# Attention scores, q times k transposed: the stores move from SyncE's queue to ScalarE's

## Chip, cores, metric

One Trainium2 chip, one core of it. The metric is the device time of one execution in microseconds (us), as a median of several executions. The core's span in the profile is some 1.9 us shorter than the device time. The TensorE clock granted in the profiled runs at full size was 0.77 to 0.86 of full speed.

## The reference

```python
# q, k: [8, 8, 512, 64] float32
scale = 1.0 / np.sqrt(64)
return (np.einsum('bhqd,bhkd->bhqk', q, k) * scale).astype(np.float32)   # [8, 8, 512, 512]
```

It reads 16.8 MB and writes 67.1 MB.

## The kernel before

The 8 x 8 heads are done in 4 units of 16 heads. Each unit loads k and q (two DMAs of 2.1 MB), GpSimd casts them to bf16, TensorE transposes them, and 4 output tiles of 4.2 MB are computed. A tile is eight pairs of matmuls into PSUM, evacuated in turn by ScalarE and VectorE into one big SBUF buffer, and then one store. Three big buffers serve the loads and the output tiles alike; so the fourth load waits for a cast, and the third output tile waits for the cast of the fourth load.

```python
big_pool = ctx.enter_context(tc.tile_pool(name="big", bufs=3))
psum_pool = ctx.enter_context(tc.tile_pool(name="psum", bufs=2, space=bass.MemoryType.PSUM))
...
def evacuate(dst, src):                       # pinned: keeps the program's order on its engine
    if n_evac % 2 == 0:
        pinned(nc.scalar.mul(out=dst, in_=src, mul=scale))
    else:
        pinned(nc.vector.tensor_scalar(out=dst, in0=src, scalar1=scale, ...))
...
def load_and_cast(v):
    xf = big_pool.tile([P, 2, 2, J * D], f32, name="big")
    for x, src in enumerate((k_r, q_r)):
        nc.sync.dma_start(out=xf[:, x], in_=src[v]...)
    ...                                       # four casts on GpSimd
...
def scores(v, t):
    kT, qz = ts[v]
    o = big_pool.tile([P, 2, RO, S], f32, name="big")
    for x in range(2):
        for i in range(0, RO, 2):
            ps = psum_pool.tile([P, 2, S], f32, name="ps")
            ...                               # two matmuls
            evacuate(o[:, x, i:i + 2, :], ps)
            yield
    nc.sync.dma_start(out=out_r[v, t], in_=o.rearrange("p x i k -> p x (i k)"))
...
cast = [load_and_cast(v) for v in range(UNITS)]   # all loads are first in the order
```

## Time and profile before

| | before |
|---|---|
| device time, median (range) | 202.59 us (202.53 to 202.62) |
| span in the profile | 200.7 us |
| busiest compute engine | VectorE, 53% of the span |
| data queue q1 | 98.3% of 16 DMA engines' span |
| DMA rate over the span | 418 GB/s |

In the profile's page, a line of a group gives busy time, mean and the idle time before it. A wait line gives total us, number and longest. A queue line gives packets, MB and the share of the 16 DMA engines' time that its packets took. The lines on which the argument rests are in the prediction below.

### The profile page before, as it was taken

The page shows a single profiled execution, that of the slowest core. Times are in us where ns is not written, and L with a number is a line of the kernel's source. Part 1 is how long each engine was busy: PE and PEld are TensorE (multiplying, and loading weights), DVE is VectorE, ACT ScalarE, POOL GpSimd, SP SyncE. Part 2 cuts the span into 40 slices and gives each one's busy share as a digit, 9 for nine tenths or more (in the row PEclk, how much of TensorE's full clock was granted, in tenths as well). Part 3 has the DMA queues.
Part 4 walks back from the last instruction along what each step waited for, and adds up shares of the span by engine and source line. Part 5 has one row for each costly group of instructions (what it writes and reads, how often), then busy time and mean ns, then how long its engine had stood idle before and what let it go on. Part 6 is the DMA issues. An engine that isn't in the chain of part 4 may idle for free.

```text
span 200.7 us, 1143 instructions
## 1 busy us (share of the span) xinstructions
PE 105.3 (52%) x384; PEld 45.8 (23%) x384; DVE 106.8 (53%) x98; ACT 85.0 (42%) x97; POOL 39.5 (20%) x22
## 2 busy tenths in 40 slices
PE   0035758566657465478637496748585667510000
PEld 0034535223214131224313122312121111100000
DVE  6705538486475976485749357844444444630000
ACT  2004423864755629253844384366435243620000
POOL 1299999995000000000000000000000000000000
PEclk9999576999699999957999759975858858975555
DMA  6999999999999999999999999999999999999994
GB/s 206 424 444 437 421 421 441 434 395 421 434 424 441 428 431 431 433 426 434 431 428 424 434 441 424 431 431 434 424 431 434 431 424 431 428 437 428 428 428 199
DMA packets 5509, 83.95 MB, mean 418 GB/s; under 512 B 384, under 2 KB 384, under 8 KB 384
## 3 DMA queue, kind: packets, MB, share of 16 engines
q1 hardware_dynamic: 5504, 83.89, 98.3%
q8 instruction: 3, 0.05, 0.1%
q14 instruction: 2, 0.02, 0.0%
HBM read 16.78 MB, written 67.11 MB: 418 GB/s over the span
## 4 chain that ended last, share of the span: by engine, by line
DMA 40%; DVE 10%; PE 8%; ACT 6%; issue 1%; ACTq 0%; SPq 0%; DVEq 0%
DMA out_dram<-big 40%; DVE big L68 9%; PE ps L141 8%; ACT big L66 5%; ACT qz L103 1%; DVE qz L103 1%; ACTq L66 0%; SPq L146 0%; DVEq L68 0%
## 5 line engine op out<-in xcount | busy, mean ns | idle before, releaser
L141 PE MATMUL ps<-kT,qz 128*128 128x512 bf16 x256 | 87.6, 447 | 55.5 <-ACT big L66 41.6
L68 DVE TENSOR_SCALAR big<-ps 128x1024 f32<-128x1024 f32 x64 | 78.4, 1224 | 59.8 <-PE ps L141 37.2
L66 ACT ACTIVATE big<-ps 128x1024 f32<-128x1024 f32 x64 | 65.5, 1023 | 73.0 <-PE ps L141 37.2
L141 PEld LDWEIGHTS <-qz 128*128 128x128 bf16 x256 | 27.2, 106 | 111.0 <-issue 97.5
L89 POOL CAST xb<-big 128x2048 bf16<-128x2048 f32 x16 | 38.8, 2468 | 7.9 <-DMA big<-in_k_dram 7.3
L117 PE MATMUL tp<-identity,xb 128*128 128x128 f32 x64 | 11.6, 346 | 13.4 <-POOL xb L89 13.4
L103 ACT COPY kT<-tp 64x512 f32<-64x512 f32 x16 | 9.2, 577 | 15.3 <-PE tp L117 15.1
L103 DVE COPY kT<-tp 64x512 f32<-64x512 f32 x16 | 11.0, 686 | 6.3 <-PE tp L117 6.0
L117 PEld LDWEIGHTS tp<-identity,xb 128*128 128x128 f32 x64 | 10.5, 184 | 15.2 <-POOL xb L89 13.4
L103 DVE COPY qz<-tp 64x512 f32<-64x512 f32 x16 | 11.0, 687 | 2.7 <-PE tp L125 2.5
L103 ACT COPY qz<-tp 64x512 f32<-64x512 f32 x16 | 9.6, 602 | 2.9 <-PE tp L125 2.7
L125 PE MATMUL tp<-identity,xb 128*128 128x128 f32 x64 | 9.4, 300 | 2.5 <-ACT kT L103 2.5
L125 PEld LDWEIGHTS tp<-identity,xb 128*128 128x128 f32 x64 | 8.5, 156 | 4.3 <-issue 3.3
L156 DVE MEMSET qz<- 128x4096 uint32 x2 | 6.9, 3472 | 2.5 <-PEq L184 1.7
L103 ACT ACT_TABLE_LOAD x1 | 1.3, 1283 | 0.7 <-PEq L184 0.7
masks.py:199 POOL TENSOR_SCALAR_AFFINE_SELECT identity<-identity 128x128 f32<-128x128 f32 x1 | 0.3, 292 | 0.1
masks.py:197 POOL MEMSET identity<- 128x128 f32 x1 | 0.2, 204 | 0.3 <-POOLq L184 0.3
L184 POOL MEMSET const-float32-0.0<- 128x1 f32 x1 | 0.1, 98 | 0.2 <-issue 0.2
L184 POOL MEMSET const-bfloat16-1.0<- 128x1 bf16 x1 | 0.1, 101 | 0.0
L184 POOL MEMSET const-uint8-127<- 128x1 uint8 x1 | 0.1, 101 | 0.0
L184 POOL MEMSET const-float32-1.0<- 128x1 f32 x1 | 0.1, 98 | 0.0
## 6 DMA issues: line engine op xcount, KB each, us to landing
out_dram<-big SPq DMA_DIRECT2D x16, 4096.0 KB, 20.7
big<-in_k_dram SPq DMA_DIRECT2D x4, 2048.0 KB, 18.1
big<-in_q_dram SPq DMA_DIRECT2D x4, 2048.0 KB, 22.7
```

The source lines that it names most:

```text
L66: pinned(nc.scalar.mul(out=dst, in_=src, mul=scale))
L68: pinned(nc.vector.tensor_scalar(out=dst, in0=src, scalar1=scale, scalar2=None, op0=mybir.AluOpType.mult))
L89: pinned(nc.gpsimd.tensor_copy(out=xb[:, :, s].rearrange("p (g i) d e -> p g e i d", i=wide), in_=xf[:, x, s].rearrange("p (g e i d) -> p ...
L103: pinned(copy(out=dst(s, h), in_=src[:, h]))
L117: pinned(nc.tensor.transpose(out=tp[:, j, :], identity=identity, in_=kb[:, j0 + j]))
L125: pinned(nc.tensor.transpose(out=tp[:, i, jj, :], identity=identity, in_=qb[:, RO * jj + i0 + i]))
L141: pinned(nc.tensor.matmul(out=ps[:, w, :], lhsT=qz[:, i + w, n, :], rhs=kT[:, n].rearrange("d m s j -> d (m s j)"), start=True, stop=True))
L156: nc.vector.memset(qz, 0.0)
L184: nc = _bacc.Bacc("TRN2", target_bir_lowering=False, num_devices=1)
```

## The change

The intent is to give the stores a hardware queue of their own, so that they don't stand behind the loads, and to let an engine issue them that has just finished its own part of the tile.

```diff
@@ def scores(v, t):
                 evacuate(o[:, x, i:i + 2, :], ps)
                 yield
-        nc.sync.dma_start(out=out_r[v, t], in_=o.rearrange("p x i k -> p x (i k)"))
+
+        pinned(nc.scalar.dma_start(out=out_r[v, t], in_=o.rearrange("p x i k -> p x (i k)")))
```

## The prediction

> **What bounds the kernel now.** I read the page's slices and queues first, then the stretches, then the waits of the two queues concerned, and last the timeline of the stretch in which loads and stores meet. The strip of 40 slices and the queue table:
>
> ```profile
> DMA  6999999999999999999999999999999999999994
> GB/s 206 424 444 437 421 421 441 434 395 421 434 424 441 428 431 431 433 426 434 431 428 424 434 441 424 431 431 434 424 431 434 431 424 431 428 437 428 428 428 199
> ...
> q1 hardware_dynamic: 5504, 83.89, 98.3%
> ```
>
> The reader should see that the DMA engines have work in every slice, that only the first and last slices are partly empty, and that all loads and stores go through one hardware queue, q1. No compute engine is above 53% of the span. Next, the stretches (columns: length, busy time and count of PE, PEld, DVE, ACT, POOL, then clock, DMA share, GB/s):
>
> ```profile
> 0.00:5.00 5.00, 0.00 (x0) 0.00 (x0) 3.34 (x1) 1.28 (x1) 0.70 (x6) 1.00 0.63 206
> 5.00:41.00 36.00, 18.41 (x80) 12.45 (x81) 17.94 (x20) 12.90 (x18) 32.02 (x14) 0.86 1.01 430
> 41.00:198.00 157.00, 86.88 (x304) 33.38 (x303) 85.52 (x79) 70.83 (x79) 6.78 (x3) 0.81 1.00 429
> 198.00:200.70 2.70, 0.00 (x0) 0.00 (x0) 0.00 (x0) 0.00 (x0) 0.00 (x0) 0.50 0.10 42
> ```
>
> Loads (mostly before 41 us) and stores (after) move at the same 430 and 429 GB/s, at a full DMA share. The time is bytes over rate: 83.89 MB / 0.430 MB per us = 195 us, plus about 1.5 us before the first packet, 2.5 us after the last, and some 1.7 us of small dips. One 4.19 MB store takes 9.75 us of the engines, one 2.10 MB load 4.88 us. Then the waits, first on SyncE's queue, then on ScalarE (total us, times, longest):
>
> ```profile
> SPq L146 <- DVE big L68: 152.5, 16, 17.6
> ...
> ACT big L66 <- DMA out_dram<-big: 31.3, 12, 3.5
> ```
>
> SyncE issues each store as soon as VectorE finishes a tile's last evacuation; it blocks nobody while it waits. ScalarE waits 12 times, 2.6 us in the mean, for a store to give back one of the three big buffers: that is the DMA pushing back on the compute. It shows that a small delay of ScalarE has somewhere to vanish.
>
> **What the Trainium skill says.** DMA: Bandwidth & Descriptors, section "Issuing engines are not separate DMA queues": DMAs of any issuing engine run on the same 16 DMA engines and interleave, and issuing from several saves only sequencer time. The trace cannot test the interleaving (it has one data queue), but the sequencer time it would save is small here: 0.37 us per store on a SyncE that is idle otherwise. The same page, "Queues, rings and completion order": each DMA engine takes turns between the queues that have work, one packet at a time. No run of before shows it; my main risk rests on it. The same page, "Where 436 GB/s comes from", has 435 GB/s as the fabric ceiling; 430 GB/s measured agrees, and says that no reordering of queues has much above it to gain. Perfetto Trace Analysis, "DMA Instruction — HWDGE (DVE, Sync)": the reported time of such an instruction ends when the sequencer is free, without the data movement. The trace agrees: 0.37 us on SyncE against a median of 20.7 us to landing. So ScalarE would be held for tenths of a microsecond per store, not for ten.
>
> **The change part by part.**
>
> *Removed:* nothing from the DMA engines; the same 16 stores in the same form. SyncE loses 16 issues, of no worth, because it is on no path.
>
> *Added on ScalarE:* 16 issues at SyncE's 0.37 us (I assume the same on ScalarE), 6 us on an engine that is busy for 85 of 201 us. And each issue must wait in ScalarE's program order for VectorE's eighth evacuation of the tile, so ScalarE's first evacuation of the next tile can no longer run ahead of it. In the timeline of before it does so at a few places: ScalarE begins an evacuation at 63.63 us while that tile's predecessor is stored at 64.24. Cost there: 0.61 + 0.37, about 1 us of ScalarE. In the steady part it is hidden: the store at 91.97 us would free ScalarE at about 92.35, and its next evacuation starts at 92.72 anyway, on a landing. Even an unhidden microsecond does not reach the DMA: the median store needs 20.7 us to land for 9.75 us of data, so about one whole store is queued ahead of it.
>
> *Moved:* the order in which bytes go. Now store 0 is issued at 36.81 us behind the last loads and must let them finish. On its own queue it starts at once and shares the engines with them. Here are the stores, and the last load's cast with what follows it:
>
> ```profile
> 36.81 0.40 SPq L146 DMA_DIRECT2D out_dram<-big  x1
> ...
> 47.49 0.39 SPq L146 DMA_DIRECT2D out_dram<-big  x1
> ...
> 56.55 0.37 SPq L146 DMA_DIRECT2D out_dram<-big  x1
> ...
> 64.24 0.37 SPq L146 DMA_DIRECT2D out_dram<-big  x1
> ```
>
> ```profile
> 43.17 4.86 POOL L89 CAST xb<-big 128x2048 bf16<-128x2048 f32 x2 [0.26 <-DMA big<-in_q_dram]
> ...
> 48.07 1.02 ACT L66 ACTIVATE big<-ps 128x1024 f32<-128x1024 f32 x1 [3.44 <-PE ps L141]
> 48.16 1.22 DVE L68 TENSOR_SCALAR big<-ps 128x1024 f32<-128x1024 f32 x1 [0.74 <-POOL xb L89]
> ```
>
> GpSimd casts the last load (q of unit 3) as soon as it lands; the third output tile takes that load's buffer, so both evacuating engines start it at 48.07, when the cast ends at 48.03. Landings, from the DMA view of narrow windows: the last k load 18.33 + 19.6 = 37.9, the last q load 18.70 + 24.3 = 43.0, store 0 36.81 + 17.1 = 53.9, store 1 47.49 + 16.0 = 63.5.
>
> Now the sum for after. ScalarE has copies until 37.16 in its order ahead of the first issue, so store 0 goes out at about 37.2; its first packet follows some 0.75 us later (the first load is issued at 0.74 us and the DMA share begins near 1.5), so 37.95. The last q load has 43.0 - 37.95 = 5.05 us of transfer left. At half rate it takes 10.1 us and lands at 48.0 instead of 43.0. Its two casts (4.86 us) end at about 52.9 instead of 48.03, and tile 2 starts 4.9 us later. It took 56.55 - 48.07 = 8.5 us to fill, so its store is issued at about 61.4 and has packets at 62.2. Store 0 and the load together have the same bytes as before, so store 0 lands at 53.9 still and store 1 at 63.5. The last store of all is issued at 178.1 and lands 21.8 us later, 199.9, while the packets end near 198.2, so a landing is some 1.6 us behind the last packet and the queue runs dry at 63.5 - 1.6 = 61.9. **The gap: 62.2 - 61.9 = 0.3 us.** The reserve of store 2 (before: 61.9 - 57.3 = 4.6 us) is just used up. After that it grows back: tiles fill in 7.7 to 8.7 us and a store takes 9.75, about 1 to 2 us per tile, and tile 3's store, issued at about 69.7, has until 72.0. At the end the last store is still behind a full queue, so the end moves by the gap alone.
>
> The sum: 202.6 + 0.3 = **202.9 us**.
>
> **The rivals.**
> (A) *The turns are not equal.* If stores get two packets to the load's one, the load needs 3 x 5.05 = 15.1 us and lands near 53, tile 2's store comes near 66.4 with packets at 67.2, and the DMA engines starve for about 5 us: 208 us, 2.5% slower. For it: nothing in the trace; against: loads and stores have packets of one size (5504 packets for 83.89 MB, of which 384 are tiny, so 16 KB each), and an equal turn of equal packets is an equal share. If the load is favoured, or stays first because descriptors are served in the order of issue, nothing is lost: 202.6 us.
> (B) *ScalarE becomes the bound.* It would take an issue that holds it for several microseconds, or its wait for VectorE falling on the path. For it: the waits column of SyncE is long (152.5 us), and the waiting now happens on a working engine. Against: nearly all of that is simply the time in which VectorE and ScalarE fill the tile together; ScalarE adds to its own work only the last evacuation of VectorE, at most 1.2 us, plus 0.37 us, per 9.75 us tile. Even wholly exposed, 8.7 + 1.6 = 10.3 us per tile for the longest fills alone would cost about 0.5 us each for some of 16: 204 to 206 us.
> (C) *A mixture of reads and writes moves faster*, since the two directions might overlap in an engine. At most the 5 us of overlap would shrink, by perhaps 1 us: 201.7 us. Against: 430 GB/s in both directions, near the ceiling named above. A store that starts earlier is by itself no gain, because the DMA engines had no gap to fill there.
>
> **Range and chances.** The central case is 202.9. Down to 201.9 for (C), up to 204.8 for an unequal share or some exposed ScalarE delay. The limits at 2% are 198.5 and 206.7: the first needs 4 us that no gap of the DMA strip offers (chance 0.01); the second needs most of (A) or all of (B) (0.05). Same: 0.94.
>
> **What would show it.** Right: two data queues, with 16.8 and 67.1 MB; DMA share at 9 in all inner slices, at most a slight dip near 60 to 65 us; the last q load landing near 48, its casts ending near 53, store 2 issued near 61.4; ScalarE's issues of about 0.4 us; its waits for landings a little shorter, with the store issues in them; mean DMA rate still near 418 GB/s. Wrong: a last load that lands at 43 (no sharing) or past 50 (unequal), a hole in the DMA strip in the steady part, a tile period above 9.75 us with ScalarE's wait for VectorE on the chain, or a rate in the shared stretch clearly above 430 GB/s.

## The result, and the profile after

| | before | after |
|---|---|---|
| device time, median (range) | 202.56 us (202.41 to 202.62), 4 runs | 203.01 us (202.94 to 203.07), 4 runs |
| span in the profile | 200.7 us | 201.2 us |
| last q load: issue to landing | 18.70 + 24.3 = 43.0 | 18.78 + 26.8 = 45.6 |
| casts of the last q load end | 48.03 | 50.62 |
| store 0, 1, 2, 3 issued at | 36.81, 47.49, 56.55, 64.24 | 36.66, 48.53, 59.38, 67.50 |

Executions over 1.5% slower than the fastest of the same kernel are left out of the means. The ratio is 1.0023, with a 95% interval of 1.0006 to 1.0041: the same within 2%, but a little slower, clear of the noise. Ratios here are the mean time of one kernel's fast runs over that of the other's of the same rounds, so they are not quite the ratios of the medians.

The strip and the queue table of the page after the change:

```profile
DMA  6999999999999999999999999999999999999993
GB/s 205 430 449 420 427 443 430 404 414 433 414 433 446 423 417 446 435 415 436 440 423 417 446 433 420 433 440 430 417 433 446 417 420 453 427 417 427 427 446 156
...
q10 hardware_dynamic: 4352, 67.11, 78.0%
q1 hardware_dynamic: 1152, 16.78, 20.2%
```

There are two data queues now, and the strip is as full as before. The stretch in which I had feared a hole, after the change (length, busy time and count of each engine, clock, DMA share, GB/s):

```profile
50.00:56.00 6.00, 3.77 (x8) 1.07 (x8) 2.45 (x2) 5.04 (x7) 0.61 (x1) 0.54 1.00 423
56.00:62.00 6.00, 3.60 (x13) 1.15 (x12) 3.67 (x3) 2.38 (x4) 0.00 (x0) 0.89 1.02 437
62.00:68.00 6.00, 4.28 (x22) 2.07 (x21) 3.67 (x3) 3.03 (x4) 0.00 (x0) 1.00 1.02 437
```

No hole: 437 GB/s on both sides of 62 us. The cast of the last q load, and ScalarE's own timeline with its queue (ACTq), after the change:

```profile
45.77 4.85 POOL L89 CAST xb<-big 128x2048 bf16<-128x2048 f32 x2 [2.80 <-DMA big<-in_q_dram]
```

```profile
36.66 0.42 ACTq L147 DMA_DIRECT2D out_dram<-big  x1
38.00 1.02 ACT L66 ACTIVATE big<-ps 128x1024 f32<-128x1024 f32 x1 [1.29 <-POOL xb L89]
...
48.53 0.38 ACTq L147 DMA_DIRECT2D out_dram<-big  x1
50.65 1.02 ACT L66 ACTIVATE big<-ps 128x1024 f32<-128x1024 f32 x1 [5.08 <-POOL xb L89]
...
59.38 0.38 ACTq L147 DMA_DIRECT2D out_dram<-big  x1
59.86 1.02 ACT L66 ACTIVATE big<-ps 128x1024 f32<-128x1024 f32 x1 [1.46 <-DVE big L68]
```

Two things are to be seen. GpSimd now waits 2.80 us for the load instead of 0.26, and tile 2 starts at 50.65 instead of 48.07. And behind store 2, ScalarE's next evacuation has waited 1.46 us for VectorE: it is held by the issue that stands ahead of it. The waits of ScalarE after the change show how often:

```profile
ACT big L66 <- DMA out_dram<-big: 13.5, 6, 2.9
ACT big L66 <- DVE big L68: 11.3, 6, 2.5
ACT big L66 <- POOL xb L89: 9.4, 3, 5.1
```

Before, ScalarE waited 31.3 us in 12 waits for landings. Now it waits six times for landings and six times for VectorE's last evacuation, 24.8 us together. By these numbers one wait has taken the place of the other, and the DMA rate is the same.

**Which engine ends last.** Each of the 16 DMA engines ends its part of a transfer with a 4-byte packet, so the trace gives 16 end times for each transfer. I took the median and the last of them, for the last load, for store 0 and for the last store (us from the span's start):

| run | last q load: median, last | store 0: median, last | last store: median, last | span |
|---|---|---|---|---|
| before | 42.25, 42.67 | 51.97, 53.39 | 198.09, 199.49 | 200.7 |
| after | 44.03, 45.27 | 51.98, 53.66 | 198.07, 199.98 | 201.2 |

The median DMA engine ends at the same time in both kernels. The 0.5 us lie in the one engine that ends last. It is not one and the same engine throughout. After the change, the engine that is last at store 0 (53.66) can be followed through its packets in steps of 9.72 us to 150.85, at store 10; there another one is already later, at 151.06. The last engine is behind that of the kernel before by 0.27 us at store 0, 0.18 at store 8 and 0.49 at the end. So in this trace part of the 0.5 us arises long after the last load. The experiments ask where the cost comes from.

### The profile page after: what moved, and what is told of

The parts are those of the page before. It is cut to its first block, busy times and chain, and to the rows that moved or that the text cites. A ratio compares the mean times of both kernels' runs of the same rounds, so it can differ in the third digit from the quotient of the medians.

```text
span 201.2 us, 1129 instructions
## 1 busy us (share of the span) xinstructions
PE 103.5 (51%) x384; PEld 44.7 (22%) x384; DVE 106.8 (53%) x98; ACT 85.0 (42%) x97; POOL 39.5 (20%) x22
## 5 line engine op out<-in xcount | busy, mean ns | idle before, releaser
L117 PE MATMUL tp<-identity,xb 128*128 128x128 f32 x64 | 9.8, 308 | 13.5 <-POOL xb L89 13.5
L117 PEld LDWEIGHTS tp<-identity,xb 128*128 128x128 f32 x64 | 9.1, 164 | 15.0 <-POOL xb L89 13.5
L125 PE MATMUL tp<-identity,xb 128*128 128x128 f32 x64 | 10.2, 317 | 2.5 <-ACT kT L103 2.5
L125 PEld LDWEIGHTS tp<-identity,xb 128*128 128x128 f32 x64 | 9.2, 165 | 4.1 <-POOL xb L89 2.7
```

Of the source, the lines that this page charges most:

```text
L117: pinned(nc.tensor.transpose(out=tp[:, j, :], identity=identity, in_=kb[:, j0 + j]))
L125: pinned(nc.tensor.transpose(out=tp[:, i, jj, :], identity=identity, in_=qb[:, RO * jj + i0 + i]))
```

## The experiments

Theory S: the cost comes from store 0 and the last load sharing the DMA engines. Rival I: it comes from ScalarE's issues in the other 15 tiles. Rival L: it is only the accident of which DMA engine is last.

### Store 0 alone, and all but store 0, from ScalarE

```diff
-        nc.sync.dma_start(out=out_r[v, t], ...)
+        if v == 0 and t == 0:          # the second run: if (v, t) != (0, 0)
+            pinned(nc.scalar.dma_start(out=out_r[v, t], ...))
+        else:
+            nc.sync.dma_start(out=out_r[v, t], ...)
```

> Only store 0 goes out from ScalarE; the other 15 stay on SyncE. The change costs 0.45 us (203.01 against 202.56). If that cost comes from the stretch in which loads and stores share the DMA engines, this run has all of it: 203.0 us, last q load landing near 45.6 as in the changed kernel. If it comes from ScalarE issuing in the steady part, this run has none: 202.55 us. If it is only which DMA engine happens to be last (in the changed kernel the slowest engine ends 1.9 us after the median engine, before 1.4 us, the medians being equal at 198.1), the time is anything from 202.3 to 203.3 and follows that distance.

> Store 0 stays on SyncE behind the loads; the other 15 go out from ScalarE. Sharing theory: the last q load lands at 43.0 as before, store 2 is issued near 57, 202.55 us. ScalarE-issue theory: 203.0 us. Last-engine theory: 202.3 to 203.3, following the distance of the slowest DMA engine from the median one. In all three the 15 issues lengthen ScalarE's tile in the unhidden places by some 0.4 us each without moving the end.

Measured, five runs each: store 0 alone 203.15 us (202.66 to 203.27), ratio to before 1.0021 (1.0008 to 1.0035). All but store 0: 202.56 us (202.35 to 202.72), ratio 0.9998 (0.9985 to 1.0012).

| run | last q load: median, last | store 0: median, last | last store: median, last | span |
|---|---|---|---|---|
| store 0 alone | 44.01, 44.90 | 52.34, 54.36 | 198.41, 200.18 | 201.4 |
| all but store 0 | 42.14, 42.55 | 51.86, 53.22 | 198.06, 199.38 | 200.6 |

The cost is there with store 0 alone and gone with the other fifteen, so I falls. L as a mere accident is unlikely, because the time follows the place of store 0. S fits, but these two runs show only that the cost goes with store 0's queue, not that the sharing makes it. How the cost shows differs too. With store 0 alone, the median engine is already 0.37 us late at the end of store 0 (52.34 against 51.97) and stays so; in the changed kernel only the last one is late.

The median's part can be read from the packets. In each run some 16 KB packets of the loads are slow in the 6 us after store 0's issue. The table has what those over 0.65 us took beyond the usual 0.61, per DMA engine, and the end of store 0 (the last two runs follow below; one trace each):

| run | slow packets, us per engine | store 0, median end |
|---|---|---|
| before | 0.37 | 51.97 |
| after | 0.40 | 51.98 |
| store 0 alone | 0.66 | 52.34 |
| all but store 0 | 0.26 | 51.86 |
| tiny early store | 0.79 | 52.37 |
| later place | 0.46 | 52.07 |

The two columns differ from before by the same amounts within 0.1 us, so by these traces the slow packets account for the delay of the median engine. They are there before the change too, and why they are slow is open.

### Is a new queue slow to start?

In the changed kernel store 0 is issued at 36.66, but its first packet starts at 40.46. The DMA view of two windows, by queue, after the change, the first 37 to 40 us and the second 40 to 43:

```profile
q1 hardware_dynamic: 74, 1.16, 97.6%
```

```profile
q1 hardware_dynamic: 42, 0.69, 60.1%
q10 hardware_dynamic: 31, 0.51, 39.5%
```

For over three microseconds after the issue the store's queue q10 moves nothing. The next experiment uses ScalarE's queue once, early, with a tiny store to a scratch tensor:

```diff
+    scratch = nc.dram_tensor("scratch", [P, 16], bf16, kind="Internal").ap()
+    pinned(nc.scalar.dma_start(out=scratch, in_=qzs[1][:, 0, 0, :16]))
```

> The changed kernel with one tiny store (32 bytes of each of 128 rows to a scratch tensor) issued from ScalarE near 9 us, so that its queue has been used before store 0. In the changed kernel store 0 is issued at 36.66 and its first packet starts only at 40.46, 3.8 us later, so the load lost 2.6 us and not the 5 I predicted. If a first use of the queue costs those 3 us, the first packet of store 0 now starts within 1 us of its issue, near 37.5, and the last q load lands near 48. If what was already handed to the DMA engines goes first, the first packet still starts near 40.5 and the load lands near 45.6. Time 203.0 in the second case, up to 203.3 in the first.

Measured: 202.99 us (202.55 to 203.14), ratio 1.0013 (0.9999 to 1.0026). Store 0 was issued at 37.43 and its first packet started at 41.69, 4.3 us later; the last load's cast began at 45.27. So it is not the first use of the queue. Nor is ScalarE's queue slow by itself: with two big buffers (a run below), when all loads have landed, store 0 is issued at 46.76 and its first packet starts at 47.70, 0.94 us later.

### An early store beside a deep queue of loads

```diff
+    scratch = nc.dram_tensor("scratch", [P, RO * N * P], bf16, kind="Internal").ap()
+    pinned(nc.scalar.dma_start(out=scratch, in_=qzs[1].rearrange("p i n q -> p (i n q)")))
```

> The changed kernel with an extra store of 2.10 MB (16 KB of each of 128 rows to a scratch tensor) issued from ScalarE near 9.4 us, when SyncE's queue holds some 9.5 MB of loads. Time: 2.10 MB / 0.430 = 4.9 us more, 207.9, in every theory. Where its packets lie tells how the two queues take turns. Equal turns at once: first packet near 10.5, last near 20.3. A fixed amount already handed to the DMA engines goes first (some 5 to 6 packets of 0.61 us each, as at store 0), then equal turns: first packet near 13.2, last near 23. Order of issue across the queues: first packet near 31, after all loads issued before it.

Measured: 207.94 us (207.82 to 208.04), as expected from 4.9 us more of bytes. The store was issued at 9.44, its first packet started at 13.17, its last transfer packet was done by 24.02. The DMA view of 9.5 to 13 us, then of 13 to 23 us:

```profile
q1 hardware_dynamic: 93, 1.36, 103.7%
```

```profile
q1 hardware_dynamic: 152, 2.15, 51.6%
q10 hardware_dynamic: 136, 2.10, 48.9%
```

This settles how the queues take turns here. For 3.7 us only the loads run, some six packets of 0.61 us for each DMA engine. After that the turns are equal, 51.6% to 48.9%. It is neither equal turns at once, as I had predicted, nor the order of issue, with which the store's first packet would have come near 31 us. In the changed kernel the last load had some 5.6 us of packets left when store 0 was issued at 36.66 (before, its median engine ends at 42.25). Of these 3.8 us ran undisturbed, and the other 1.8 took twice as long: the median engine ended 1.8 us later, at 44.03. The last engine, and with it the landing, came 2.6 us later, not the 5.0 of the prediction.

### When compute sets the pace

The DMA bound hides ScalarE's part. To see it bare, I halved the stores (output wrong: half of it is not written), from SyncE and from ScalarE:

```diff
-  .dma_start(out=out_r[v, t], in_=o.rearrange("p x i k -> p x (i k)"))
+  .dma_start(out=out_r[v, t][:, 0], in_=o[:, 0].rearrange("p i k -> p (i k)"))
```

> The kernel before, but each store writes only the first half of its tile (2.10 MB; half of the output stays unwritten, wrong on purpose). The DMA engines then need 50.3 MB / 0.430 = 117 us and compute sets the pace: store 0 still near 36.8, then 15 tiles at the 7.7 to 8.5 us that a fill takes, 36.8 + 15 x 8.1 = 158, plus some 7 us of the last store and 2 outside the span: about 167 us. If fills themselves are paced by landings and are shorter when unhindered, less, down to 155.

> The changed kernel with the same half stores. In its full-size trace an unhindered tile took 8.12 us from store issue to store issue against 7.69 before, and the next 9.23 against 8.53: 0.43 to 0.70 us more. If ScalarE's issue with its wait for VectorE is a real cost that only the DMA bound hides, this run is 15 x 0.43 to 0.70 = 6 to 10 us slower than the half stores from SyncE, about 3 to 6%. If ScalarE's issue costs nothing by itself, the two are equal.

Measured, in fast runs: from SyncE 163.29 and 163.77 us (two other runs, of 168.1 and 168.3 us, were slow, and the profile is of one of them); from ScalarE 178.12 and 180.05 us (two others, of 181.2 and 184.5 us, were slow). Over the full-size kernel before, the ratios are 0.8072 and 0.8840, so ScalarE's is 0.8840 / 0.8072 = 1.095 times SyncE's. That is more than the 3 to 6% expected, and the reason given there is not what the trace shows. A half store needs only the first four evacuations (store 0 from SyncE goes out at 32.40 here, against 36.81 for the whole one), and they are long done; ScalarE's timeline has the issue 0.06 us behind the start of an evacuation, and beside it:

```profile
99.77 1.02 ACT L66 ACTIVATE big<-ps 128x1024 f32<-128x1024 f32 x1 [0.47 <-PE ps L141]
99.83 0.34 ACTq L147 DMA_DIRECT2D out_dram<-big  x1
```

So ScalarE does not wait for VectorE's last evacuation there. By the traces, store 2 goes out 4.2 us later (55.59 against 51.40); the last q load, which shares the engines with the stores, lands at 48.0 instead of 43.0. From store 2 to store 15 the tiles take (171.17 - 55.59) - (159.22 - 51.40) = 7.8 us longer, 0.6 us each. (One trace is fast, the other slow; the slow one is the quicker kernel, so the sign is safe and the size is not.) I first thought of the place of the issue in ScalarE's order and moved it behind the next tile's first evacuation:

```diff
-        pinned(nc.scalar.dma_start(...))      # at the end of the tile
+                if (x, i) == (0, 0):
+                    store()                   # the tile before, behind this tile's first evacuation
```

> Half stores from ScalarE, each placed one evacuation later in ScalarE's order: behind the first evacuation of the next tile. Half stores from ScalarE were 15 us (9%) slower than from SyncE in fast runs; in the traces 4.2 us of it lie before store 2 (loads and stores share the engines and tile 2 waits for the last load's casts) and 0.6 us in each later tile. If the 0.6 us come from where the issue stands between ScalarE's evacuations, this run loses only the early part: some 168 us. If they come from ScalarE issuing at all, it stays near 179 us.

> The half stores from SyncE once more, for a profile in the fast state (the first one fell in a run of 168.1 us while the fast ones took 163.3 and 163.8) and on the chip of the two other runs: 163.5 us in fast runs, with a tile every 7.7 to 9.3 us.

Measured in fast runs: the later place 186.8 to 188.9 us (one slow run of 191.6), ratio 0.9251; SyncE again 162.9 and 163.6 us, ratio 0.8056 (two slow runs of 166.1 and 167.5; its profile is one of them again). The later place is not better but worse, 1.148 times SyncE's: my expectation missed on both branches. The last experiment leaves the half stores on SyncE and adds a tiny store on ScalarE in the same place of its order, from a constant tile:

```diff
         nc.sync.dma_start(out=out_r[v, t][:, 0], ...)
+        pinned(nc.scalar.dma_start(out=scratch[v * TILES + t], in_=identity[:, :4]))
```

> Half stores from SyncE as before, and after each of them a tiny store (16 bytes of each of 128 rows of a constant tile) issued from ScalarE in the place where the changed kernel has its store. It takes the same kind of issue on ScalarE (some 0.34 us of its sequencer) but depends on no evacuation and frees no buffer. The half stores from ScalarE were 15 us slower than from SyncE, the later place 24 us slower. If an issue on ScalarE by itself disturbs the alternation of the two evacuating engines, this run is slow too, 172 us or more. If what the store waits for or what it moves in the order of loads and stores is the cost, it stays at the 163.5 us of the half stores from SyncE.

Measured in fast runs: 163.72 and 165.26 us (two slow ones of 167.3 and 168.4), ratio 0.812 (0.8075 to 0.8166), as SyncE alone. So an issue of this length in ScalarE's order costs nothing measurable here by itself. The real store differs in more: it shares with the loads, and it leaves later in its tile than SyncE's does (at 99.83, some 2.6 us after the end of the fourth evacuation). The same late moment from SyncE was not tried. What the real store's issue on ScalarE does to a compute-bound kernel stays open; what the traces show is that both evacuating engines wait longer for TensorE. These are the half stores from SyncE (a slow run), then from ScalarE:

```profile
ACT big L66 <- PE ps L141: 47.9, 46, 2.1
...
DVE big L68 <- PE ps L141: 33.2, 42, 1.8
```

```profile
ACT big L66 <- PE ps L141: 59.8, 51, 2.8
DVE big L68 <- PE ps L141: 44.2, 44, 3.4
```

The granted clock differed too (0.96 and 0.98 in SyncE's two fast runs of the first call, 0.92 and 0.93 in ScalarE's, 0.85 to 0.87 with the later place). The clock alone does not explain the difference: ScalarE's fast run of 178.1 us at 0.93 is 10 us longer than SyncE's slow ones of 168.1 and 168.3 us at 0.90 and 0.89. Whether the rest of the clock's difference is a cause or a consequence, the runs can't tell.

### Without the reserve of a queued store

Whole stores again, but two big buffers instead of three, from SyncE and from ScalarE:

```diff
-    big_pool = ctx.enter_context(tc.tile_pool(name="big", bufs=3))
+    big_pool = ctx.enter_context(tc.tile_pool(name="big", bufs=2))
```

> The kernel before with two big buffers instead of three: no store is queued ahead. Tile 0 must wait for the casts of the third load (near 38 us), store 0 near 46.5, and each tile then costs a fill (7.7 to 8.5 us) plus issue-to-packet (0.75) plus the landing behind the last packet (1.6), about 10.4 us instead of 9.75: 47 + 16 x 10.4 + 2 = 215 us, with holes in the DMA strip.

> The changed kernel with two big buffers. If the reserve of a queued store is what hides ScalarE's 0.4 to 0.7 us per tile, this run is 15 x 0.4 to 0.7 = 6 to 10 us slower than two buffers with SyncE. If the wait for the buffer's landing hides it (ScalarE issues about 1.5 us before the landing that lets it go on anyway), the two are equal within 1 us, near 215 us.

Measured: from SyncE 216.59 us (215.92 to 217.55), from ScalarE 218.31 us (218.15 to 218.90). The ratios to before are 1.0695 and 1.0786, so ScalarE's is 1.0085 times SyncE's, about 1.8 us. (It is not the clock: SyncE's runs at the lowest, 0.77 and 0.78, took 215.9 and 217.2 us.) It lies between the two theories and nearer to the second: most of ScalarE's delay falls into the wait for the landing, a rest of about 0.1 us per tile does not. ScalarE's waits for landings, of the two in the same order:

```profile
ACT big L66 <- DMA out_dram<-big: 44.6, 14, 4.7
```

```profile
ACT big L66 <- DMA out_dram<-big: 44.5, 14, 5.3
```

ScalarE waits as long and as often for the landing, whoever issues. With the third buffer back, the same difference of 1.8 us is gone, as the run with all stores but store 0 on ScalarE shows (202.56 against 202.53 us).

### A later place at full size

> The changed kernel at full size with the same later place of the issue. Where DMA sets the pace the place does not matter: 203.0 us as the changed kernel, 202.5 if the later store 0 (issued at about 39 instead of 36.7, so less sharing) takes back what the sharing cost.

Measured: 202.80 us (202.55 to 203.51), ratio 1.0021 (1.0001 to 1.0041). It can't be told from the changed kernel nor, within some tenths, from before. It shares less: store 0 is issued at 37.83, its first packet starts at 41.87, and the median engine ends the last q load at 42.94 (44.03 in the changed kernel, 42.25 before). Yet the mean is not lower, so the cost does not visibly follow the length of the sharing. No version here is faster than the kernel before. With a DMA strip that is full from end to end, none was expected to be by much.

## Why the prediction was right, point by point

- **The bound.** Right. The DMA engines move 83.9 MB at 430 GB/s in both kernels; the rates of the stretch from 80 to 198 us are 429 and 429 GB/s.
- **ScalarE's issue takes 0.37 us.** Right: 0.38 us for most, 0.42 for the first.
- **The issue holds ScalarE until VectorE is done, and that is hidden.** Right, and more frequent than "a few places": six waits of 11.3 us. The run with all but store 0 on ScalarE shows it costs nothing at the end; that the third buffer's reserve is what hides the last of it is shown by the pair with two buffers.
- **Store 0 "starts at once and shares the engines".** Wrong. It starts 3.8 us after its issue and only then takes equal turns, as the early store shows with 3.7 us and 51.6% to 48.9%. So every time that followed was too late: the last q load landed at 45.6 and not at 48.0, its casts ended at 50.62 and not at 52.9, store 2 was issued at 59.38 and not at 61.4. The fill of tile 2 itself took 59.38 - 50.65 = 8.7 us for the 8.5 I used.
- **The gap of 0.3 us.** Wrong. The queue does not run dry: by the median engine store 1 ends at 61.70 and store 2 has been issued 2.3 us before that. Two readings were loose as well. The 5.05 us that the load was to have left run to its landing at 43.0, not to its last packets at 42.25 to 42.67; and the landing 1.6 us "behind the last packet" holds for the median engine only: before the change the last engine ends at 199.49, 0.4 us before the landing at 199.9.
- **The sum, 202.9 us.** Right in size, 203.01 measured, and right that nothing big would move; that its last term fits is luck. The 0.3 us of starving did not happen, and in their place there are 0.45 us that come with store 0 on the second queue, as the run with store 0 alone shows. That the sharing itself makes them is not shown. With store 0 alone and with the tiny early store the median engine ends 0.3 us late, by slow packets; in the changed kernel only the DMA engine that ends last is late, and why is open.
- **Rival (A), unequal turns.** The turns are unequal at the beginning, in the load's favour, so nothing starved. **Rival (B)** happened off the path that sets the end. **Rival (C)**, a faster mixture: no. From 40 to 43 us the changed kernel moved 1.20 MB, the kernel before 1.13; over 36 to 48 us the two are within 1%.

## What to carry to other kernels

The DMA strip here was full from end to end, and moving the stores to another queue only changed the order of the bytes. In such a case look first for a hole that the move could fill, and if there is none, expect little. Then look at what the reordering delays: the load that shared with a store landed 2.6 us later, and store 2, which waited for its buffer, went out 2.8 us later, of 4.6 us of reserve. Letting an engine that computes issue the stores was safe here while the DMA engines set the pace; with half stores, where they did not, the same move cost 9%, for reasons that stay open.

## What the Trainium skill lacked or had wrong

- DMA: Bandwidth & Descriptors, "Queues, rings and completion order" has the engines take turns between queues by packets. True here (51.6% to 48.9%) only after the first 3.4 to 4.3 us: until then a store issued on a second queue beside queued loads moved nothing, while some six 16 KB packets of the loads ran on each engine. The page does not have this head start.
- The same page, "Issuing engines are not separate DMA queues", says that issuing from several engines saves sequencer time. It has nothing on what the move of the issues to a computing engine can cost: 9.5% in the run with half stores. The sequencer time alone is not the reason, since a tiny store in the same place cost nothing there (0.812 against 0.8056).
- No page that I read has a 16 KB instruction packet holding back the data of one DMA engine. Before the change the last engine is behind the median one by 0.42 us at the last load, 1.42 us at store 0 and 1.40 us at the end. An instruction packet of 0.96 us, at 48.4 us, lies within store 0, and the data packet that starts as it ends took 0.98 us instead of 0.61. With two big buffers from SyncE, where the queues run empty between stores, the lag is 0.07 to 0.24 us, but 0.9 to 1.9 us at stores 4, 6, 7, 12 and 13; instruction packets lie at 95 to 99, 116.4 and 177.7 us, within stores 4, 6 and 12. That they cause the lag fits each time, but no run was made without them.
- No page that I read has the slow packets at the turn from loads to stores: 18 to 31 packets of 0.65 to 1.35 us instead of 0.61, within some 4 us, 0.26 to 0.79 us per engine by run, 0.37 before the change and 0.40 after. They begin 1.5 to 3.2 us after a store is issued while loads still run (at 39.5, 39.1 and, with the early store, 11.6 us), and are missing with two big buffers, where no load was left. Why is open.
